# Raw weight buffers and the order of the seven-product steps in the MLP of a hybrid decoder layer

## The chip, the cores and the metric

The kernel runs on one core of one Trainium2 chip. The metric is device time in microseconds (us), smaller is better. The time before is 1105.0 us, the median of three runs (1101.55 to 1105.72).

A core has a matrix engine (PE in the profile; its weight loads are shown as PEld), three engines for elementwise work (DVE, the vector engine; ACT, the scalar engine; POOL), and SP, which here only issues DMA transfers from the chip's memory into SBUF. Every engine runs its own list of instructions strictly in the order of that list; engines wait for each other with semaphores. Matmul results go to PSUM, which has eight banks of 128 x 512 float32.

## The reference, cut to what matters

One decoder layer over 256 tokens of width 2048 in float32. The mixer (a Mamba-2 part and a sparse attention part between one input and one output projection) comes first; the change touches only what follows it:

```
u = rmsnorm(x, g_mlp) @ w_up                  # 256 x 2048 @ 2048 x 8192
return x + jnp.square(jax.nn.relu(u)) @ w_down  # 256 x 8192 @ 8192 x 2048
```

## The kernel before, in words

**Precise products.** Every float32 matrix is split into a rounded high part and a remainder, and a product is three matmuls: high by high, low by high, high by low (`three`, L186 to L192). Weights come from memory as a *raw* tile of 512 KB (128 partitions x 1024 values); ACT casts it to the high part (L144) and DVE subtracts to get the low part (L145). Both parts lie in one tile of the tag `w2`, which has `WB = 5` buffers; raw tiles have `RB = 4`. A raw buffer is free for the next load when DVE has subtracted; a `w2` buffer is free when PE has used it.

**Stages of the MLP.** The 8192 hidden columns are 32 groups of 256, worked off in three parts of 11, 11 and 10 groups (`PARTS`). For each part `up` computes the hidden values (PE line L230, "acc<-x2x,w" in the profile), squares them and splits them into `uh` and `ul`; then `down` multiplies them by `w_down`, in two halves `j` of 1024 output columns each. A half is a loop over the part's groups; one pass is a *step* here. A step needs two raw tiles (the quarters b11, b21 and b12, b22 of a 256 x 1024 block of `w_down`) and accumulates a 2 x 2 grid of PSUM banks.

**Plain and seven-product steps.** A plain step has eight products of 128x128 by 128x512, so 24 matmuls. In the steps listed in `SEVEN` Strassen's scheme (in Winograd's form) is used: seven products, 21 matmuls. For it POOL forms four combinations of the raw quarters (L852 to L855, one after another, one of them in place in the second raw tile); ACT then casts and DVE subtracts the two raw tiles (L860, L861) and the three other combinations, tile `t` (L863, L864), which become tile `wt`. `SEVEN = {2, 4, 6}` gives three such steps in each half, 18 of the 64 steps. Four products of a seven-product step go to four more banks (p1, p5, p6, p7); behind the last such step of a half ACT copies p1 (L913) and DVE adds these banks into the residual `xr` (L886 and L915 to L921). The eight banks are two tags of four, and the next half uses them the other way round: its grid takes the banks of p1, p5, p6 and p7.

**Order.** The order of PE's instructions is the order of the program text. For the other engines a scheduler sets it by a model of costs; everything inside `tc.high_priority(offset=HP)`, which holds the loads, casts, subtractions and combinations of weights, is pulled far ahead of its place. A buffer's reuse makes waits in that order: a load waits for the subtraction that frees its raw buffer, a cast for the matmul that frees its `w2` buffer.

**The start of the MLP.** The last residual of the mixer is transposed on PE (L694, tile ps_sr) and split by ACT (L697) and DVE (L698) into `x2x` while the first product of `up` already runs; ACT also squares the rows into scratch tiles (`junk`, L787). When the mixer's scratch pool `mid` is closed, the pool `mlp` takes its place in SBUF.

Of the kernel before, what the change touches and what calls it, by code (L numbers as in the profile page):

```python
# [9 lines left out]
F32 = mybir.dt.float32  # L10
F32R = mybir.dt.float32r
I32 = mybir.dt.int32
AF = mybir.ActivationFunctionType
OP = mybir.AluOpType
AX = mybir.AxisListType

P = 128
# [10 lines left out]
HP = 600  # L28
WARM = 9
WB = 5  # L30
RB = 4


SPARE = 64
SHIFT = 16
# [7 lines left out]
FIRST_W = 32  # L43


PARTS = (0, 11, 22, 32)
SEVEN = {2, 4, 6}

A11, A21, A12, A22 = range(4)
S3, S1, S2, S4 = 1, 4, 5, 6  # L50
# [34 lines left out]
def hymba_kernel(ctx: ExitStack, tc: tile.TileContext, xn, xt, w_in, w_out, w_up, w_down, vcol, vrow, out):  # L85
    nc = tc.nc
# [39 lines left out]
        return vc[:, VC[name] + i:VC[name] + i + 1]  # L126


    def operands(src, n, load=None, shift=0, parts=2):

        pitch = (n + 63) // 64 * 64
        with tc.high_priority(offset=HP):
            raw = wts.tile([P, parts, pitch], F32, name="raw", tag="raw", bufs=RB)
            both = wts.tile([P, 2 * parts * pitch + SPARE], F32R, name="w2", tag="w2", bufs=WB)
            hi, lo = (both[:, shift + i * parts * pitch:shift + (i + 1) * parts * pitch]
                      .rearrange("p (k c) -> p k c", k=parts)[:, :, :n] for i in range(2))
            src = src.rearrange("p (k c) -> p k c", k=parts)
            step = parts if load is None else 1
            for i in range(0, parts, step):
                s = slice(i, i + step)  # L140
                nc.sync.dma_start(raw[:, s, :n], src[:, s])
                if load is not None:
                    load()
                nc.scalar.copy(hi[:, s], raw[:, s, :n])  # L144
                nc.vector.tensor_tensor(lo[:, s], raw[:, s, :n], hi[:, s].bitcast(F32), op=OP.subtract)  # L145
        return hi, lo
# [663 lines left out]


    mlp = ctx.enter_context(tc.tile_pool(name="mlp", bufs=2))

    def up(h, tag):

# [18 lines left out]
            u.append((uh, ul))  # L834
        return u

    def weights(j, g, seven):


        if not seven:  # L840
            ops = [operands(w_down[2 * j + c, g], 512, shift=SHIFT) for c in range(2)]
            return [[(ops[c][0][:, k], ops[c][1][:, k]) for c in range(2)] for k in range(2)]
        with tc.high_priority(offset=HP):
            raws = []
            for c in range(2):
                raws.append(wts.tile([P, 2, 512], F32, name="raw", tag="raw", bufs=RB))
                nc.sync.dma_start(raws[c], w_down[2 * j + c, g].rearrange("p (k c) -> p k c", k=2))
            both = mlp.tile([P, 2 * 3 * 512 + SPARE], F32R, name="wt")
            th, tl = (both[:, SHIFT + i * 1536:SHIFT + (i + 1) * 1536].rearrange("p (k c) -> p k c", k=3) for i in range(2))
            t = mlp.tile([P, 3, 512], F32, name="t", bufs=1)  # L850

            nc.gpsimd.tensor_tensor(t[:, 0], raws[1][:, 1], raws[1][:, 0], op=OP.subtract)  # L852
            nc.gpsimd.tensor_tensor(raws[1][:, 0], raws[1][:, 0], raws[0][:, 0], op=OP.subtract)  # L853
            nc.gpsimd.tensor_tensor(t[:, 1], raws[1][:, 1], raws[1][:, 0], op=OP.subtract)  # L854
            nc.gpsimd.tensor_tensor(t[:, 2], raws[0][:, 1], t[:, 1], op=OP.subtract)  # L855
            ops = []
            for raw in raws:
                w2 = wts.tile([P, 2 * 2 * 512 + SPARE], F32R, name="w2", tag="w2", bufs=WB)
                hi, lo = (w2[:, SHIFT + i * 1024:SHIFT + (i + 1) * 1024].rearrange("p (k c) -> p k c", k=2) for i in range(2))
                nc.scalar.copy(hi, raw)  # L860
                nc.vector.tensor_tensor(lo, raw, hi.bitcast(F32), op=OP.subtract)  # L861
                ops.append((hi, lo))
            nc.scalar.copy(th, t)  # L863
            nc.vector.tensor_tensor(tl, t, th.bitcast(F32), op=OP.subtract)  # L864
        pick = lambda o, k: (o[0][:, k], o[1][:, k])
        (b11, b21), (t1, b22) = ([pick(o, k) for k in range(2)] for o in ops)
        t3, t2, t4 = (pick((th, tl), k) for k in range(3))
        return b11, b21, b22, t1, t2, t3, t4

    def down(h, u, tags):  # L870
        pairs = len(u)
        marked = SEVEN
        for j in range(2):
# [18 lines left out]
            kept = []  # L892
            for g in range(pairs):
                seven = g in marked
                w = weights(j, PARTS[h] + g, seven)
                if seven:
                    b11, b21, b22, t1, t2, t3, t4 = w
                    new = ps7 is None
# [10 lines left out]
                    go(acc[1][0], u[g], A22, t4, False)  # L909
                    if done:  # L910

                        s1 = mlp.tile([P, 512], F32, name="s1", bufs=1)
                        nc.scalar.copy(s1, p1)  # L913
                        add(0, half[0], p1)
                        nc.vector.tensor_tensor(s1, s1, p6, op=OP.add)  # L915
                        s2 = mlp.tile([P, 512], F32, name="s2", bufs=1)
                        nc.vector.tensor_tensor(s2, s1, p7, op=OP.add)
                        add(1, half[0], s2)
                        nc.vector.tensor_tensor(s1, s1, p5, op=OP.add)
                        add(0, half[1], s1)  # L920
                        nc.vector.tensor_tensor(s2, s2, p5, op=OP.add)  # L921
                        add(1, half[1], s2)
# [87 lines left out]
```

## Time and profile before

One execution was profiled. Its own time was 1102.39 us, its span 1100.6 us.

| what | number |
|---|---|
| three runs, median | 1105.0 us |
| the profiled execution | 1102.39 us, span 1100.6 us |
| PE busy | 1070.3 us, 97% |
| DVE, ACT, POOL busy | 746.4, 551.0, 123.5 us |
| mean granted TensorE clock | 0.990 |
| down stages, from first to last matmul | about 501.9 to 628.0, 745.3 to 873.2 and 979.9 to 1097.0 us |

How to read it: in rows of waits the first name is who waited, behind the arrow what ended the wait, then the total, the number of times and the longest, in us. In rows of groups: line, engine, operation, output<-inputs, shapes, count, then busy us and the mean ns of one, then the idle time of the engine before them with its releaser. In a timeline: start, duration, engine, line, operation, and in brackets the idle time before it. In rows of stretches: the stretch, its length, then busy time and count of instructions of each engine asked for, the granted clock (1.00 is full), the share of the DMA engines in use, GB/s. Matmuls overlap: one of 512 columns is shown with 0.38 us, though the next starts 0.22 us after it. The ends of matmuls are modelled.

### The profile page before, as it was taken

How to read it: one execution, taken by the hardware profiler on the slowest of the kernel's cores; microseconds unless marked ns; L12 is line 12 of the kernel's file. 1: busy time of each engine (PE TensorE's matmuls, PEld its weight loads, DVE VectorE, ACT ScalarE, POOL GpSimd, SP SyncE). 2: the span in 40 equal slices, each digit the busy share in tenths (PEclk: the TensorE clock that was granted, in tenths of full speed). 3: DMA queues.
4: the chain of work that ended last, by engine and by line, in shares of the span. 5: the costliest groups of instructions: out<-in, count | busy, mean ns of one | idle time of the engine just before them, and what ended most of it. 6: DMA issues, size and time to landing. Idle time of an engine off the chain costs nothing.

```text
span 1100.6 us, 15648 instructions
## 1 busy us (share of the span) xinstructions
PE 1070.3 (97%) x5962; PEld 938.7 (85%) x5962; DVE 746.4 (68%) x1066; ACT 551.0 (50%) x749; POOL 123.5 (11%) x102
## 2 busy tenths in 40 slices
PE   9999999999999999999898999999998999998988
PEld 8999998888888898988686889897786888987876
DVE  6787997687665576764674767765665767754846
ACT  7755555567654554553544445544344445544433
POOL 0020000221000000003123000004123000023140
PEclk9999999999999999999999999999899999999999
DMA  9865437544565556664554766663554666645753
GB/s 329 261 213 182 158 105 241 172 135 135 165 236 187 187 185 201 196 197 150 186 178 161 242 207 195 194 207 134 192 186 169 226 202 192 198 147 172 239 163 115
DMA packets 63611, 207.41 MB, mean 188 GB/s; under 512 B 7088, under 2 KB 11440, under 8 KB 63536
## 3 DMA queue, kind: packets, MB, share of 16 engines
q1 hardware_dynamic: 63392, 206.36, 57.5%
q8 instruction: 47, 0.77, 0.3%
q14 instruction: 28, 0.23, 0.1%
q10 hardware_dynamic: 144, 0.05, 0.0%
HBM read 204.29 MB, written 2.10 MB: 188 GB/s over the span
## 4 chain that ended last, share of the span: by engine, by line
PE 73%; POOL 9%; DMA 5%; DVE 5%; issue 4%; ACT 4%; POOLq 0%; ACTq 0%; DVEq 0%
PE acc L230 29%; PE acc L192 10%; PE acc L209 10%; PE acc L189 10%; PE acc L191 10%; DMA raw<-in_w_down 5%; POOL raw L853 2%; DVE w L861 2%; POOL t L854 2%; POOL t L852 2%; POOL t L855 2%; ACT wt L863 2%; DVE w L145 2%; ACT w L144 2%; PE ps_y L610 1%
## 5 line engine op out<-in xcount | busy, mean ns | idle before, releaser
L145 DVE TENSOR_TENSOR w<-raw,w 128x1024 fp32r<-128x1024 f32 (+3 forms) x364 | 420.2, 1166 | 204.0 <-ACT w L144 203.1
L144 ACT CAST w<-raw 128x1024 fp32r<-128x1024 f32 (+3 forms) x364 | 357.5, 993 | 335.8 <-PE acc L192 104.7
L230 PE MATMUL acc<-x2x,w 128*128 128x512 f32 (+2 forms) x2053 | 343.0, 327 | 0.0
L230 PEld LDWEIGHTS acc<-x2x,w 128*128 128x128 f32 x2053 | 307.9, 188 | 34.4
L192 PE MATMUL acc<-w,uh 128*128 128x512 f32 (+1 forms) x444 | 171.9, 387 | 15.6 <-DVE w L861 15.6
L189 PE MATMUL acc<-w,uh 128*128 128x512 f32 (+5 forms) x459 | 171.4, 379 | 10.0 <-ACT w L860 10.0
L191 PE MATMUL acc<-w,ul 128*128 128x512 f32 (+1 forms) x444 | 169.4, 382 | 0.0
L209 PE MATMUL acc<-hx,w 128*128 128x256 f32 (+1 forms) x978 | 115.0, 277 | 0.0
L192 PEld LDWEIGHTS acc<-w,uh 128*128 128x128 f32 x444 | 83.7, 189 | 35.2 <-DVE w L861 21.0
L209 PEld LDWEIGHTS acc<-hx,w 128*128 128x128 f32 x978 | 112.7, 188 | 0.0
L189 PEld LDWEIGHTS acc<-w,uh 128*128 128x128 f32 x459 | 86.2, 188 | 29.2 <-ACT w L860 14.4
L864 DVE TENSOR_TENSOR wt<-t,wt 128x1536 fp32r<-128x1536 f32 x18 | 31.7, 1759 | 114.9 <-ACT wt L863 114.9
L852 POOL TENSOR_TENSOR t<-raw 128x512 f32<-128x512 f32 x18 | 24.7, 1373 | 716.5 <-DMA raw<-in_w_down 669.1
L191 PEld LDWEIGHTS acc<-w,ul 128*128 128x128 f32 x444 | 83.7, 188 | 14.4
L863 ACT CAST wt<-t 128x1536 fp32r<-128x1536 f32 x18 | 26.5, 1474 | 128.9 <-POOL t L855 128.9
L189 PE MATMUL acc<-w,hx 128*128 128x512 f32 (+3 forms) x228 | 83.9, 371 | 0.0
L191 PE MATMUL acc<-w,hx 128*128 128x512 f32 (+1 forms) x224 | 80.9, 361 | 0.0
L192 PE MATMUL acc<-w,hx 128*128 128x512 f32 (+1 forms) x224 | 80.7, 360 | 0.0
L189 PEld LDWEIGHTS acc<-w,hx 128*128 128x128 f32 x228 | 43.0, 189 | 6.1 <-issue 0.7
L191 PEld LDWEIGHTS acc<-w,hx 128*128 128x128 f32 x224 | 42.4, 189 | 5.9 <-issue 0.7
L192 PEld LDWEIGHTS acc<-w,hx 128*128 128x128 f32 x224 | 42.2, 189 | 6.0 <-DVE w L145 0.4
L861 DVE TENSOR_TENSOR w<-raw,w 128x1024 fp32r<-128x1024 f32 x36 | 46.1, 1279 | 0.2 <-ACT w L860 0.2
(229 smaller groups left out, 1033.3 us busy)
## 6 DMA issues: line engine op xcount, KB each, us to landing
raw<-in_w_up SPq DMA_DIRECT2D x128, 512.0 KB, 4.1
raw<-in_w_down SPq DMA_DIRECT2D x128, 512.0 KB, 4.3
raw<-in_w_in SPq DMA_DIRECT2D x72, 512.0 KB, 3.5
raw<-in_w_out SPq DMA_DIRECT2D x32, 512.0 KB, 3.3
raw<-in_w_in SPq DMA_DIRECT2D x16, 256.0 KB, 5.2
raw<-in_w_in SPq DMA_DIRECT2D x16, 152.0 KB, 5.2
raw<-in_w_in SPq DMA_DIRECT2D x8, 304.0 KB, 3.2
xT<-in_xt SPq DMA_DIRECT2D x8, 256.0 KB, 5.2
```

What stands on the lines that cost most here:

```text
L144: nc.scalar.copy(hi[:, s], raw[:, s, :n])
L145: nc.vector.tensor_tensor(lo[:, s], raw[:, s, :n], hi[:, s].bitcast(F32), op=OP.subtract)
L189: nc.tensor.matmul(go(out[:, i:j]), ah, go(wh[:, i:j]), start=first and i == 0, stop=False, skip_group_check=True)
L191: nc.tensor.matmul(go(out), al, go(wh), start=False, stop=False, skip_group_check=True)
L192: nc.tensor.matmul(go(out), ah, go(wl), start=False, stop=last, skip_group_check=True)
L209: nc.tensor.matmul(acc[:, c, at:at + n], w[:, 0, s], x[:, fr:fr + n], start=(i + k + j == 0), stop=(i >= 2 and k == 7 and j == len(todo) - ...
L230: nc.tensor.matmul(walk(out[:, at:at + n]), w[:, 0, s], walk(x[:, at:at + n]), start=(i < 2 and k + j == 0), stop=(i >= 2 and k == 7 and j ...
L852: nc.gpsimd.tensor_tensor(t[:, 0], raws[1][:, 1], raws[1][:, 0], op=OP.subtract)
L853: nc.gpsimd.tensor_tensor(raws[1][:, 0], raws[1][:, 0], raws[0][:, 0], op=OP.subtract)
L861: nc.vector.tensor_tensor(lo, raw, hi.bitcast(F32), op=OP.subtract)
L863: nc.scalar.copy(th, t)
L864: nc.vector.tensor_tensor(tl, t, th.bitcast(F32), op=OP.subtract)
```

## The change

- `SEVEN` becomes {2, 5, 8}, so two plain steps stand between seven-product steps. `PARTS` becomes (0, 10, 21, 32): parts of 10, 11 and 11 groups. There are still 18 seven-product and 46 plain steps.
- Once the pool `mlp` exists, raw tiles are taken in turn from the old four buffers and from four new ones (tag `rawm`) in `mlp`.
- `weights` is divided. `combine` loads the two raw tiles of a seven-product step and forms the combinations on POOL; it is called one step ahead, before the loads of the plain step in front. `combined` does the casts and subtractions, at the step itself.
- To make room `wt` has one buffer in place of two, and `s1`, `s2` take the two buffers of `up`'s tile `r`.

```diff
-PARTS = (0, 11, 22, 32)
-SEVEN = {2, 4, 6}
+PARTS = (0, 10, 21, 32)
+SEVEN = {2, 5, 8}
...
+    mlp_pool = []
+    taken = [0]
+
+    def raw_tile(parts, pitch):
+
+        taken[0] += 1
+        pool, tag = (mlp_pool[0], "rawm") if mlp_pool and taken[0] % 2 else (wts, "raw")
+        return pool.tile([P, parts, pitch], F32, name="raw", tag=tag, bufs=RB)
+
     def operands(src, n, load=None, shift=0, parts=2):
...
-            raw = wts.tile([P, parts, pitch], F32, name="raw", tag="raw", bufs=RB)
+            raw = raw_tile(parts, pitch)
...
     mlp = ctx.enter_context(tc.tile_pool(name="mlp", bufs=2))
+    mlp_pool.append(mlp)
...
+    def combine(j, g):
+
         with tc.high_priority(offset=HP):
             raws = []
             for c in range(2):
-                raws.append(wts.tile([P, 2, 512], F32, name="raw", tag="raw", bufs=RB))
+                raws.append(raw_tile(2, 512))
                 nc.sync.dma_start(raws[c], w_down[2 * j + c, g].rearrange("p (k c) -> p k c", k=2))
...
             t = mlp.tile([P, 3, 512], F32, name="t", bufs=1)
...
+        return raws[0], raws[1], t
+
+    def combined(raws):
+
+        ops = []
+        with tc.high_priority(offset=HP):
             for raw in raws:
...
+                    both = mlp.tile([P, 2 * 3 * 512 + SPARE], F32R, name="wt", bufs=1)
...
                 nc.scalar.copy(hi, raw)
                 nc.vector.tensor_tensor(lo, raw, hi.bitcast(F32), op=OP.subtract)
...
-                w = weights(j, PARTS[h] + g, seven)
+
+                if g + 1 in marked:
+                    ahead = combine(j, PARTS[h] + g + 1)
+                w = combined(ahead) if seven else plain(j, PARTS[h] + g)
...
-                        s1 = mlp.tile([P, 512], F32, name="s1", bufs=1)
+                        s1, s2 = (mlp.tile([P, 7, P], F32, name="r")[:, :4].rearrange("p k t -> p (k t)")
+                                  for _ in range(2))
                         nc.scalar.copy(s1, p1)
                         add(0, half[0], p1)
                         nc.vector.tensor_tensor(s1, s1, p6, op=OP.add)
-                        s2 = mlp.tile([P, 512], F32, name="s2", bufs=1)
```

The change moves instructions at three places of which the prediction speaks. Numbers in names tell buffers and tiles apart.

**ACT, the second seven-product step of a part's first half** (step 4 before, step 5 now). Before; w2_5240 and w2_5245 are the plain step 3, w2_5283, wt_5277 and w2_5286 the seven-product step 4, w2_5313 the plain step 5:

```order
L144 CAST w2_5240<-raw_5239 128x1024
L144 CAST w2_5245<-raw_5244 128x1024
L860 CAST w2_5283<-raw_5273 128x1024
L863 CAST wt_5277<-t_5278 128x1536
L860 CAST w2_5286<-raw_5275 128x1024
L144 CAST w2_5313<-raw_5312 128x1024
```

Now; w2_5144 and w2_5149 are step 3, w2_5187 and w2_5192 step 4, the next three step 5, w2_5251 the plain step 6:

```order
L153 CAST w2_5144<-raw_5143 128x1024
L153 CAST w2_5149<-raw_5148 128x1024
L153 CAST w2_5187<-raw_5186 128x1024
L153 CAST w2_5192<-raw_5191 128x1024
L879 CAST w2_5220<-raw_5177 128x1024
L879 CAST wt_5226<-t_5181 128x1536
L879 CAST w2_5223<-raw_5179 128x1024
L153 CAST w2_5251<-raw_5250 128x1024
```

The cast to `wt` still stands between the two other casts of its step, but now two plain steps lie ahead of it; it waits for POOL as before, and also for PE's last use of the one `wt` buffer, in step 2.

**SP and ACT, the start of the MLP.** raw_4002 to raw_4090 are the four tiles of `up`'s first product; raw_4150, 4171, 4192 and 4213 those of its second. SP before:

```order
L141 DMA raw_4090<-in_w_up 128x1024 [waits DMAHW1_49,DVE_49]
L141 DMA raw_4150<-in_w_up 128x1024 [waits DMAHW2_49,DVE_49]
L141 DMA raw_4171<-in_w_up 128x1024 [waits DMAHW3_49,DVE_49]
L141 DMA raw_4192<-in_w_up 128x1024 [waits DMAHW4_49,DVE_49]
L141 DMA raw_4213<-in_w_up 128x1024 [waits DMAHW5_49,DVE_49]
```

SP now; the ACT semaphore that raw_4150 waits for is reached by the second of the two squarings (junk2_4067, L796):

```order
L150 DMA raw_4090<-in_w_up 128x1024 [waits DMAHW1_49,DVE_49]
L150 DMA raw_4171<-in_w_up 128x1024 [waits DMAHW2_49,DVE_49]
L150 DMA raw_4213<-in_w_up 128x1024 [waits DMAHW3_49,DVE_49]
L150 DMA raw_4267<-in_w_up 128x1024 [waits DMAHW4_49,DVE_49]
L150 DMA raw_4309<-in_w_up 128x1024 [waits DMAHW5_49,DVE_49]
L150 DMA raw_4150<-in_w_up 128x1024 [waits PE_49,Activation_49,Pool_49]
```

ACT now, from these squarings on:

```order
L796 ACTIVATE junk2_4065,ss2_3350<-xr_3345 128x512
L796 ACTIVATE junk2_4067,ss2_3350<-xr_3345 128x512
L706 ACTIVATE x2x_3547<-ps_sr_4024,vc_86 128x256 x2
L153 CAST w2_4151<-raw_4150 128x1024
L153 CAST w2_4172<-raw_4171 128x1024
L153 CAST w2_4193<-raw_4192 128x1024
L706 ACTIVATE x2x_3547<-ps_sr_4047,vc_86 128x256 x2
```

The first loads into the new buffers, raw_4150 and raw_4192, stand behind the end of the mixer's scratch pool, and on ACT the last two slices of `x2x` (from ps_sr_4047) now stand behind the casts of these two tiles. Before, all four slices stood ahead of the cast of raw_4192. DVE has the same order.

**DVE, the change of half in the first part** (10 groups; behind its last seven-product step there is one plain step, where there were four before). acc_5117 to acc_5120 are p1, p5, p6 and p7, r_5357 and r_5358 are s1 and s2; wt_5493 belongs to step 2 of the next half:

```order
L901 SCALAR_TENSOR_TENSOR xr_3345<-acc_5117,rs4_4113,xr_3345 128x512
L154 TENSOR_TENSOR w2_5416<-raw_5415,w2_5416 128x1024
L154 TENSOR_TENSOR w2_5454<-raw_5453,w2_5454 128x1024
L934 TENSOR_TENSOR r_5357<-r_5357,acc_5119 128x512
L935 TENSOR_TENSOR r_5358<-r_5357,acc_5120 128x512
L880 TENSOR_TENSOR wt_5493<-t_5448,wt_5493 128x1536
L901 SCALAR_TENSOR_TENSOR xr_3345<-r_5358,rs4_4113,xr_3345 128x512
L937 TENSOR_TENSOR r_5357<-r_5357,acc_5118 128x512
L939 TENSOR_TENSOR r_5358<-r_5358,acc_5118 128x512
```

The subtraction to `wt` of the next half stands in the middle of the chain that frees p5's bank; before, nothing stood between these adds.

More of the change, by code (lines that the diff above doesn't have):

```diff
@@ L835, in up, with plain @@
         return u
[L837 to L842, printed above, removed]
+    def plain(j, g):
+        ops = [operands(w_down[2 * j + c, g], 512, shift=SHIFT) for c in range(2)]
+        return [[(ops[c][0][:, k], ops[c][1][:, k]) for c in range(2)] for k in range(2)]
+    def combine(j, g):
         with tc.high_priority(offset=HP):
@@ L845, in weights @@
             for c in range(2):
-                raws.append(wts.tile([P, 2, 512], F32, name="raw", tag="raw", bufs=RB))
+                raws.append(raw_tile(2, 512))
                 nc.sync.dma_start(raws[c], w_down[2 * j + c, g].rearrange("p (k c) -> p k c", k=2))
-            both = mlp.tile([P, 2 * 3 * 512 + SPARE], F32R, name="wt")
-            th, tl = (both[:, SHIFT + i * 1536:SHIFT + (i + 1) * 1536].rearrange("p (k c) -> p k c", k=3) for i in range(2))
             t = mlp.tile([P, 3, 512], F32, name="t", bufs=1)
@@ L855, in weights @@
             nc.gpsimd.tensor_tensor(t[:, 2], raws[0][:, 1], t[:, 1], op=OP.subtract)
-            ops = []
+        return raws[0], raws[1], t
+    def combined(raws):
+        ops = []
+        with tc.high_priority(offset=HP):
             for raw in raws:
-                w2 = wts.tile([P, 2 * 2 * 512 + SPARE], F32R, name="w2", tag="w2", bufs=WB)
-                hi, lo = (w2[:, SHIFT + i * 1024:SHIFT + (i + 1) * 1024].rearrange("p (k c) -> p k c", k=2) for i in range(2))
+                n = raw.shape[1]
+                if n == 2:
+                    both = wts.tile([P, 2 * 2 * 512 + SPARE], F32R, name="w2", tag="w2", bufs=WB)
+                else:
+                    both = mlp.tile([P, 2 * 3 * 512 + SPARE], F32R, name="wt", bufs=1)
+                hi, lo = (both[:, SHIFT + i * n * 512:SHIFT + (i + 1) * n * 512].rearrange("p (k c) -> p k c", k=n)
+                          for i in range(2))
                 nc.scalar.copy(hi, raw)
                 nc.vector.tensor_tensor(lo, raw, hi.bitcast(F32), op=OP.subtract)
[L862 to L867, printed above, removed]
+                ops.append([(hi[:, k], lo[:, k]) for k in range(n)])
+        (b11, b21), (t1, b22), (t3, t2, t4) = ops
         return b11, b21, b22, t1, t2, t3, t4
```

## The prediction

> **What bounds the kernel now.** I read the page's engine totals first, then who waited for whom, then the down stages alone.
>
> ```profile
> PE 1070.3 (97%) x5962; PEld 938.7 (85%) x5962; DVE 746.4 (68%) x1066; ACT 551.0 (50%) x749; POOL 123.5 (11%) x102
> PE acc L192 <- DVE w L861: 15.6, 13, 1.3
> PE acc L189 <- ACT w L860: 10.0, 8, 2.2
> ACT wt L863 <- POOL t L855: 128.9, 18, 8.1
> ```
>
> PE is the bound, and nearly all of its idle time (25.6 us) stands in 21 waits for the weights of seven-product steps. A busy PE is not a PE at its pace, though, so I measure the stages by their length: the three stretches from the first to the last matmul of a down stage, and the pace of matmuls where nothing waits.
>
> ```profile
> 501.90:628.00 126.10, 117.49 (x519) 96.62 (x517) 79.04 (x76) 54.32 (x54) 32.57 (x24) 0.99 0.55 180
> 745.30:873.20 127.90, 119.97 (x519) 98.56 (x517) 79.10 (x77) 54.43 (x54) 31.89 (x23) 0.96 0.54 180
> 979.90:1097.00 117.10, 108.12 (x481) 89.14 (x479) 69.86 (x71) 45.93 (x46) 30.56 (x24) 0.97 0.49 165
> ...
> 617.23 0.39 PE L189 MATMUL acc<-w,uh 128*128 128x512 f32 x1
> ...
> 627.28 0.38 PE L189 MATMUL acc<-w,uh 128*128 128x512 f32 x1
> ```
>
> Between the two last rows lie 45 matmuls: 10.05/45 = 0.2233 us each. A part of 11 groups has 2 x (8 x 24 + 3 x 21) = 510 matmuls, 113.9 us, and 0.3 for cut first ones: 114.2. The part of 10 has 462, of which 24 are half as wide: 103.4. The stages sum to 371.1 (about 370.8 from first start to last end) where PE's pace gives 331.8: **39 us are lost there.** 25.6 is the idle time. Each of 21 restarts costs about 0.27 more (5.7): the wait is counted from an end that lies 0.16 behind the next start, and the first matmul takes 0.11 longer (0.49 below against 0.38). The remaining 7 to 8 us are the clock:
>
> ```profile
> 588.18 0.49 PE L189 MATMUL acc<-w,uh 128*128 128x512 f32 x1 [0.77 <-ACT w L860]
> 590.17 0.49 PE L192 MATMUL acc<-w,uh 128*128 128x512 f32 x1 [1.28 <-DVE w L861]
> ...
> 590.00:591.00 1.00, 0.83 (x4) 0.97 0.00 0
> 591.00:592.00 1.00, 1.00 (x4) 0.50 0.81 283
> 592.00:593.00 1.00, 1.00 (x3) 0.50 0.83 287
> ```
>
> Just behind this pair of waits the granted clock falls to 0.50, for some 3.4 us. I take it that the waits do it and that it goes with them; the other answer is a rival below.
>
> Why PE waits is read in the chain of waits and SP's timeline.
>
> ```profile
> 576.91 0.33 SPq L847 DMA_DIRECT2D raw<-in_w_down  x1
> ...
> 579.15 1.15 DVE w L861
> ...
> 580.34 1.27 POOL t L852
> ...
> 584.39 1.29 POOL t L855
> ...
> 587.09 1.04 ACT w L860
> ...
> 593.63 1.26 POOL t L852
> ```
>
> It is a loop: a raw buffer comes free late, the load takes 3.4 us (576.91 to 580.3), POOL 5.4 (580.34 to 585.7), then ACT casts `wt` and, only behind it, the second tile, which PE needs early. POOL starts its next turn 13.3 us later (580.34 to 593.63); PE's work in a turn, a seven-product and a plain step, takes (21 + 24) x 0.2233 = 10.0.
>
> **The change part by part.** Prices come from these groups.
>
> ```profile
> L145 DVE TENSOR_TENSOR w<-raw,w 128x1024 fp32r<-128x1024 f32 x324 | 396.5, 1234 | 195.9 <-ACT w L144 195.1
> L144 ACT CAST w<-raw 128x1024 fp32r<-128x1024 f32 x324 | 336.4, 1047 | 326.7 <-PE acc L192 104.7 <-issue 100.5 <-PE acc L230 50.3
> L864 DVE TENSOR_TENSOR wt<-t,wt 128x1536 fp32r<-128x1536 f32 x18 | 31.7, 1759 | 114.9 <-ACT wt L863 114.9
> L863 ACT CAST wt<-t 128x1536 fp32r<-128x1536 f32 x18 | 26.5, 1474 | 128.9 <-POOL t L855 128.9
> L853 POOL TENSOR_TENSOR raw<-raw 128x512 f32<-128x512 f32 x18 | 25.7, 1426 | 1.4
> L886 DVE SCALAR_TENSOR_TENSOR xr<-s,rs,xr 128x512 f32<-128x512 f32 x18 | 13.0, 748 | 0.2
> L917 DVE TENSOR_TENSOR s<-s,acc 128x512 f32<-128x512 f32 x6 | 4.1, 687 | 0.2
> ```
>
> *Matmuls:* 46 x 24 + 18 x 21 before and after; no gain or loss.
>
> *Buffers, look-ahead, distance:* a load now waits for the subtraction of four steps earlier, not two, and POOL starts one step sooner. Inside a half, count from the start of step 2. Its seven products end at 4.7 and step 5 begins at 15.3. The cast to `wt` for step 5 waits for 4.7 (one buffer), though POOL was done long before; 1.5 + 1.8 later the low part is there, at 8. The second tile's `w2` buffer is free at 8.7 (three quarters through step 3), so its low part is ready at 11. PE needs both between 16 and 18. At least 5 us of cover; if it goes, every us over it is a stall. Then `t` is free at 8, POOL works for step 8 until 13.4, or 16.7 if it is slowed as below, and ACT wants it at 20. So the loop is gone inside a half: **-39 us** (bounds -39 and, if one drop of the clock remains, -37).
>
> *The start of the MLP* is a new wait. These rows are ACT's second squaring, DVE's last slice of `x2x`, PE's stream, and the landing times:
>
> ```profile
> 385.60 0.19 ACT L787 ACTIVATION_READ_ACCUMULATOR junk<-xr 128x1 f32 x1
> 390.51 0.48 DVE L698 SCALAR_TENSOR_TENSOR x2x<-ps_sr,vc,x2x 128x256 fp32r<-128x256 f32 x1
> 388.39 9.96 PE L230 MATMUL acc<-x2x,w 128*128 128x32 f32 x58
> raw<-in_w_up SPq DMA_DIRECT2D x13, 512.0 KB, 3.4
> ```
>
> raw_4150 and raw_4192 are issued behind 385.8 and land 3.4 and, with 1.6 for another 512 KB, 5 us later: 389.2 and 390.8. ACT then casts three tiles (389.4 to 392.5); the third, on DVE, ends at 394.1 behind two others of 1.2. Only then come the last two slices: 0.5 each on DVE, 394.6, and behind a pass over ACT 395.5. PE reaches the first of them 21 matmuls behind 388.39, nine until the next weight tile and twelve in it, at 0.17 (9.96/58): 391.9. It stands 2.7 + 0.6: **+3.3 us** (bounds 0, if the loads land at once, and 6, if at 4.1 us and crossed), and perhaps a clock drop, +0.8 (0 to 1.7). Behind it the second product's tiles are all late by the same and no more.
>
> *The change of half in the first part.* PE needs p5's bank 1.3 us into the next half, 11.3 from the start of step 8 (4.7 + 5.3 + 1.3). That chain on DVE now holds the subtraction to `wt`. Its raw tiles take step 8's buffers. The second of these is cast when PE is three quarters through step 6, 6.7 ahead of step 8, and subtracted 2.3 later; the load lands some 4.3 later still, at about 0. POOL ends at 5.5, ACT at 7.4 with the semaphores between, DVE at 9.2; then 0.75 + 0.69 + 0.69 = 11.3. Just in time, if POOL runs undisturbed. But POOL and DVE disturb each other:
>
> ```profile
> 565.34 1.29 POOL L852 TENSOR_TENSOR t<-raw 128x512 f32<-128x512 f32 x1 [29.00 <-DMA raw<-in_w_down]
> 566.71 2.15 POOL L853 TENSOR_TENSOR raw<-raw 128x512 f32<-128x512 f32 x1
> ...
> 559.82 1.23 DVE L145 TENSOR_TENSOR w<-raw,w 128x1024 fp32r<-128x1024 f32 x1 [1.32 <-ACT w L144]
> ...
> 565.41 2.30 DVE L145 TENSOR_TENSOR w<-raw,w 128x1024 fp32r<-128x1024 f32 x1
> ```
>
> Where they meet, POOL takes 2.15 for 1.29 and DVE 2.30 for 1.23. [...] Three of four combinations slowed by 0.87 and the subtraction held up make p5 free at about 14: **+2** (0 to 4). In the other two parts two plain steps follow step 8, 5.3 us more cover; two more changes, together **+1** (0 to 3). At the end of the last half the same cover holds.
>
> *From up to down.* ACT now meets the cast to `wt` for step 2 ahead of two casts of `up`'s last product. Count from the start of the product before it; a product is four weight tiles of 2.7 us (16 matmuls at 0.17), and casts run five tiles ahead. The raw buffer that step 2 waits for is freed at 0, its load lands at 4.3, POOL ends at 10, the cast to `wt` at 11.5, the cast behind it at 12.6; on DVE that is 13.3 and 14.6. PE wants this tile, the third of the last product, at 16. ACT stands for some 6 us, but 1.4 us of cover is left. Three crossings, **+1.5** (0 to 6: 2 each if POOL is slowed). Scratch in `r` costs nothing: `up` is over, or a product of 10 us away.
>
> Sum: 1100.6 - 39 + 3.3 + 0.8 + 2 + 1 + 1.5 = 1070.2; the profiled execution lies 1.8 above its span: **1072**. It was itself 2.6 below the median shown, inside the runs' 1101.55 to 1105.72.
>
> **Rivals.** *The lock between POOL and DVE decides.* In the before POOL mostly works while ACT and DVE stand; now it works against a full stream. DVE's 228.0 us in the down stages plus 72 combinations x 1.07 is 305 of 332 us, 92%, and at each end of a half the adds come on top. Against: on average it fits, and weights are 2.5 steps ahead. If each of six halves loses 3 us: 1063.4 (1102.4 less 39) + 18 + 4.1 at the start + 1.5 at the crossings = 1087.
>
> *The clock drops are not the waits' doing* and stay: 7.5 us more, 1080. Against: each stands in or just behind a pair of waits, and long stretches without waits have none. [...]
>
> *It doesn't do what it says:* ACT still meets POOL unfinished at each of 18 `wt` casts and the loop reappears there, 39 us lost as before and 3.3 more at the start: 1106. It needs POOL 10 us later than I count; no combination took above 2.15.
>
> *Slower, by new places in SBUF:* `uh`, `ul` and `wt` lie elsewhere, and if that slowed the stage's matmuls, all 1482 would pay. For it: those on `wt` take longer even now.
>
> ```profile
> L189 PE MATMUL acc<-w,uh 128*128 128x512 f32 x421 | 162.8, 387 | 10.0 <-ACT w L860 10.0
> L189 PE MATMUL acc<-wt,uh 128*128 128x512 f32 x54 | 23.9, 443 | 0.0
> ...
> 515.47 0.38 PE L189 MATMUL acc<-wt,uh 128*128 128x512 f32 x1
> ...
> 517.45 0.38 PE L189 MATMUL acc<-w,uh 128*128 128x512 f32 x1
> ```
>
> 0.056 more on each is 83 us: 1155; it decides from 0.02 on, where it eats my 30. Against: in an undisturbed step the nine matmuls on `wt` take 1.98, 0.220 each. Their mean is long because the clock drops fall on them.
>
> **The numbers.** My forecast 0.67, the lock 0.21, the clock 0.03, no effect 0.04, slower 0.05. Forecast's own range 1063 (nothing lost) to 1082 (all upper bounds). The clock's 1080 lies in it. The range reaches to the lock, 1063 to 1091, and leaves out no effect and slower. A measurement here can tell about 0.5% from no change: faster 0.91 (the first three), same 0.04, slower 0.05.
>
> **What would show it.** Right: no wait of PE for L879/L880's products inside halves, clock 1.00 in the down stages, stages near 105, 115 and 115 us; one wait of PE near 392 for the low part of `x2x`; POOL means rising to 1.5 or more. Wrong: PE waits at every change of half (the lock), ACT idle in front of `wt` by 5 us or more (the loop), a pace above 0.23 in clean stretches (places).

## The result, and the profile after

The changed kernel takes 1065.29 us (median of 4 runs, 1064.19 to 1066.81) against 1104.4 us before (4 runs): a ratio of 0.965, 95% interval 0.9625 to 0.9675. The profiled execution is the one of 1066.81 us, with a span of 1065.0.

These are the engine totals of the changed kernel's page:

```profile
PE 1057.3 (99%) x5962; PEld 936.6 (88%) x5962; DVE 785.3 (74%) x1066; ACT 555.8 (52%) x749; POOL 151.4 (14%) x102
```

All its waits of PE, by what ended them:

```profile
PE acc L239 <- DVE x2x L707: 2.7, 2, 2.4
PE ps_w L254 <- POOL ones L249: 1.3, 1, 1.3
PE acc L198 <- ACT hx L277: 0.3, 1, 0.3
```

And its three down stages as stretches:

```profile
499.00:601.00 102.00, 102.00 (x469) 87.22 (x469) 84.02 (x71) 52.96 (x53) 36.00 (x20) 1.00 0.66 217
719.00:831.00 112.00, 112.00 (x515) 95.67 (x514) 91.73 (x77) 55.58 (x55) 35.93 (x20) 1.00 0.64 215
949.00:1061.00 112.00, 112.00 (x523) 96.02 (x523) 89.31 (x76) 51.59 (x51) 35.93 (x20) 1.00 0.54 182
```

The 21 waits for seven-product weights are gone. In the down stages PE is busy for the whole stretch, at the full clock. One new wait stands in the list, for `x2x`, and it is in the place that the prediction named: the start of the MLP. The timeline there shows ACT's casts, then a late slice of `x2x`, then PE:

```profile
390.01 2.00 ACT L153 CAST w<-raw 128x1024 fp32r<-128x1024 f32 x2 [0.49 <-DMA raw<-in_w_up]
392.54 1.04 ACT L153 CAST w<-raw 128x1024 fp32r<-128x1024 f32 x1 [0.52 <-DMA raw<-in_w_up]
393.49 0.47 ACT L706 ACTIVATE x2x<-ps_sr,vc 128x256 fp32r<-128x256 f32 x1
395.29 0.79 PE L239 MATMUL acc<-x2x,w 128*128 128x512 f32 x2 [2.44 <-DVE x2x L707]
396.31 1.01 PE L239 MATMUL acc<-x2x,w 128*128 128x512 f32 x2 [0.24 <-DVE x2x L707]
```

The two stretches around it show the granted clock, which falls to 0.50 behind the stall:

```profile
392.16:395.57 3.41, 0.97 (x6) 0.63 (x5) 2.91 (x4) 1.72 (x3) 0.00 (x0) 1.00 0.72 249
395.57:398.98 3.41, 3.17 (x10) 2.30 (x10) 1.02 (x2) 1.49 (x3) 0.00 (x0) 0.50 0.85 286
```

Where the 35.6 us between the spans (1100.6 and 1065.0) come from, by the first matmul of each stage in the two traces (the last stage up to its last matmul's start): the down stages last 101.96, 112.51 and 112.58 us, together 327.0 instead of 370.6, so -43.6. The up stages last 115.27, 117.45 and 117.45, together 350.2 instead of 342.9 for the same 32 groups, so +7.3. What lies ahead of the MLP is 0.7 longer, what lies behind it the same.

What POOL and DVE cost each other is there too. These are the groups of a seven-product step in the changed kernel: subtraction and cast of its raw tiles, POOL's second and fourth combination, cast to `wt`.

```profile
L880 DVE TENSOR_TENSOR w<-raw,w 128x1024 fp32r<-128x1024 f32 x36 | 56.4, 1566 | 20.5 <-ACT w L879 18.4 <-DMA raw<-in_w_down 1.7
L862 POOL TENSOR_TENSOR raw<-raw 128x512 f32<-128x512 f32 x18 | 32.4, 1800 | 1.4
L864 POOL TENSOR_TENSOR t<-raw,t 128x512 f32<-128x512 f32 x18 | 33.5, 1859 | 1.4
L879 ACT CAST wt<-t 128x1536 fp32r<-128x1536 f32 x18 | 26.5, 1474 | 39.8 <-POOL t L864 27.0 <-PE acc L201 12.8
```

POOL's operations take 1.8 us on average where the second took 1.43 before; DVE is busy 39 us longer than before and POOL 28, with the same instructions. None of it reaches PE. ACT's wait for POOL in front of `wt` fell from 128.9 us to 27.0.

### The profile page after: what moved, and what is told of

It is laid out like the page before. It is cut to its first block, busy times and chain, and to the rows that moved or that the text cites. A ratio compares the mean times of both kernels' runs of the same rounds, so it can differ in the third digit from the quotient of the medians.

```text
span 1065.0 us, 15655 instructions
## 1 busy us (share of the span) xinstructions
PE 1057.3 (99%) x5962; PEld 936.6 (88%) x5962; DVE 785.3 (74%) x1066; ACT 555.8 (52%) x749; POOL 151.4 (14%) x102
## 4 chain that ended last, share of the span: by engine, by line
PE 98%; DMA 1%; ACT 0%; DVE 0%; SPq 0%; issue 0%; ACTq 0%
PE acc L239 32%; PE acc L198 17%; PE acc L200 17%; PE acc L201 17%; PE acc L218 10%; PE ps_y L619 1%; DMA raw<-in_w_up 1%; PE ps_l L657 0%; PE ps_o L682 0%; PE ps_sr L703 0%; DMA xT<-in_xt 0%; PE ps_s L510 0%; PE ps_s L509 0%; PE ps_dec L610 0%; PE ps_pt L674 0%; DVE w L154 0%
## 5 line engine op out<-in xcount | busy, mean ns | idle before, releaser
L154 DVE TENSOR_TENSOR w<-raw,w 128x1024 fp32r<-128x1024 f32 (+3 forms) x364 | 439.4, 1218 | 197.0 <-ACT w L153 195.2
L153 ACT CAST w<-raw 128x1024 fp32r<-128x1024 f32 (+3 forms) x364 | 359.6, 993 | 330.4 <-PE acc L201 139.3
L239 PE MATMUL acc<-x2x,w 128*128 128x512 f32 (+2 forms) x2053 | 347.6, 330 | 2.7 <-DVE x2x L707 2.7
L198 PE MATMUL acc<-w,uh 128*128 128x512 f32 (+5 forms) x459 | 168.6, 373 | 0.0
L201 PE MATMUL acc<-w,uh 128*128 128x512 f32 (+1 forms) x444 | 168.1, 379 | 0.0
L880 DVE TENSOR_TENSOR w<-raw,w 128x1024 fp32r<-128x1024 f32 x36 | 56.4, 1566 | 20.5 <-ACT w L879 18.4
L879 ACT CAST w<-raw 128x1024 fp32r<-128x1024 f32 x36 | 37.7, 1046 | 41.9 <-PE acc L201 36.8
```

The lines of the kernel that those rows point to most:

```text
L198: nc.tensor.matmul(go(out[:, i:j]), ah, go(wh[:, i:j]), start=first and i == 0, stop=False, skip_group_check=True)
L201: nc.tensor.matmul(go(out), ah, go(wl), start=False, stop=last, skip_group_check=True)
L239: nc.tensor.matmul(walk(out[:, at:at + n]), w[:, 0, s], walk(x[:, at:at + n]), start=(i < 2 and k + j == 0), stop=(i >= 2 and k == 7 and j ...
```

## The experiments

All times stand against the kernel before, run on the same chip. "PE waits" are those in the MLP, added up from each timeline; a few tenths that the groups of waits below hold beyond them lie in the mixer.

| kernel | us | ratio, 95% interval | PE waits, us |
|---|---|---|---|
| the change | 1065.3 | 0.965 (0.9625 to 0.9675) | 2.7 |
| distance alone | 1105.4 | 0.997 (0.994 to 1.000) | 24.1 |
| the change with four raw buffers | 1087.3 | 0.982 (0.978 to 0.986) | 17.7 |
| the change without look-ahead | 1069.5 | 0.967 (0.962 to 0.971) | 5.2 |
| the change without distance | 1065.1 | 0.962 (0.958 to 0.965) | 3.4 |
| eight buffers alone | 1062.9 | 0.9615 (0.959 to 0.964) | 2.7 |
| the change, new buffers late | 1059.6 | 0.9587 (0.956 to 0.961) | 0 |
| the same, six buffers | 1063.6 | 0.962 (0.958 to 0.966) | 2.8 |
| the same, combinations on DVE | 1065.4 | 0.963 (0.960 to 0.967) | 3.6 |
| eight buffers alone, late | 1059.8 | 0.9576 (0.955 to 0.960) | 0 |
| the change, three more POOL operations a step | 1100.2 | 0.995 (0.993 to 0.997) | 22.5 |
| four seven-product steps, POOL | 1068.6 | 0.967 (0.964 to 0.970) | 8.0 |
| four seven-product steps, DVE | 1057.2 | 0.956 (0.953 to 0.959) | 0.3 |

### Distance alone

The kernel before with the new places of the seven-product steps, nothing else:

```diff
-PARTS = (0, 11, 22, 32)
-SEVEN = {2, 4, 6}
+PARTS = (0, 10, 21, 32)
+SEVEN = {2, 5, 8}
```

> The kernel before with one part of the change alone: seven-product steps 2, 5 and 8 instead of 2, 4 and 6 (and the parts' borders 10 and 21 that go with them); four raw buffers, no look-ahead. My theory (the raw buffer that is freed late is the cause, so a longer distance only lets the weights recover between two turns): the start of the MLP costs nothing, as in the kernel before; about a third to a half of the 39 us of the down stages is lost still, since the raw tiles of each seven-product step are still behind the same four buffers; 1075 to 1092 us, with waits of PE for the casts and subtractions of the halves left. Rival (distance is all that matters: the loop of 13.3 us a turn needs two turns in a row to show): no waits in the down stages, and without the 5 us at the start of the MLP 1060 to 1064 us, faster than the whole change.

1105.4 us: the rival is out, and my theory had the direction but too much effect: I gave distance half of the loss or more, and it gave 0.3%. The timeline of one seven-product step (lines of the kernel before) shows why a longer distance does not help:

```profile
516.96 1.28 POOL L855 TENSOR_TENSOR t<-raw,t 128x512 f32<-128x512 f32 x1
518.27 1.47 ACT L863 CAST wt<-t 128x1536 fp32r<-128x1536 f32 x1 [7.09 <-POOL t L855]
519.65 1.04 ACT L860 CAST w<-raw 128x1024 fp32r<-128x1024 f32 x1
521.45 1.22 DVE L861 TENSOR_TENSOR w<-raw,w 128x1024 fp32r<-128x1024 f32 x1
522.73 0.49 PE L192 MATMUL acc<-w,uh 128*128 128x512 f32 x1 [1.26 <-DVE w L861]
```

ACT, which works in order, stands 7.09 us in front of `wt`, and the step's second tile is cast behind it. It stands there for POOL at all 18 steps, 124.5 us together, against 128.9 before. That happens in each such step by itself; no second turn is needed for it. So my picture of a loop of 13.3 us against 10.0 was too narrow: the chain inside one step is late already.

### Eight buffers alone

The changed kernel with the old places of the steps, and the combinations asked for in the step itself. Against the kernel before this leaves the eight buffers (and one `wt` buffer and the scratch in `r`, which make room for them):

```diff
-PARTS = (0, 10, 21, 32)
-SEVEN = {2, 5, 8}
+PARTS = (0, 11, 22, 32)
+SEVEN = {2, 4, 6}
-                if g + 1 in marked:
-                    ahead = combine(j, PARTS[h] + g + 1)
+                if seven:
+                    ahead = combine(j, PARTS[h] + g)
```

> The kernel before with eight raw buffers alone (and the one wt buffer that makes room for them): steps 2, 4 and 6, combinations asked for in the step itself. If the buffers carry the whole gain, as the runs without look-ahead and with the old distance say: no waits for the halves, the stall near 392 us as in the changed kernel, and at most 3 us at the changes of half: 1062 to 1069 us. If look-ahead and distance stand in for each other, so that either was enough beside the buffers but not neither: the chain of load 3.4, POOL 5.4 to 7.5, cast 1.5 and subtraction 1.8 us shows at the halves again, 1072 to 1090 us.

1062.9 us: the buffers carry the whole gain. Its only waits in the MLP are the 2.7 us for `x2x`. ACT still stands in front of `wt` for POOL, 12 times and 45.9 us together, but PE feels none of it: with eight buffers the loads and combinations run early enough whichever step asks for them. What makes room for the buffers was not run alone; the next version has it with four buffers, and waits.

### Taking one part out of the change

Each of these undoes one part of the change. Four raw buffers:

```diff
-        pool, tag = (mlp_pool[0], "rawm") if mlp_pool and taken[0] % 2 else (wts, "raw")
+        pool, tag = wts, "raw"
```

> The changed kernel with all raw tiles from the four old buffers (the four of the MLP's own are left out); look-ahead and distance stay. My theory: the stall near 392 us goes (its load waited for a new buffer), which gives back 3.3 us and 1.7 us of halved clock; in exchange the raw tiles of a seven-product step now hold two of four buffers for a whole step longer, so the plain steps behind them load late: 1066 to 1085 us, with PE waits for casts of plain tiles in the down stages. Rival (the buffers are not needed once step and distance are changed): no waits in the down stages, 1060 to 1063 us.

1087.3 us, just above the range of my theory. The up stages lose nothing, the stall at the start is gone as expected, and the down stages last 352.1 us instead of 327.0:

```profile
PE acc L198 <- DVE r L939: 9.0, 1, 9.0
PE acc L201 <- DVE w L154: 7.3, 9, 1.5
PE acc L198 <- ACT w L153: 2.4, 2, 1.6
```

The waits are now for plain tiles (L153, L154), which load behind the two that the look-ahead holds, as the theory had it, and 9.0 us at the first part's change of half, which I had not expected. With distance alone the down stages last 367.8 us, 15.6 more: look-ahead, with the rewriting that comes with it, is worth that much where buffers are short.

No look-ahead:

```diff
-                if g + 1 in marked:
-                    ahead = combine(j, PARTS[h] + g + 1)
+                if seven:
+                    ahead = combine(j, PARTS[h] + g)
```

> The changed kernel with the combinations asked for in the seven-product step itself (no look-ahead); eight buffers and distance stay. My theory (buffers are the cause; the scheduler runs loads and combinations as early as buffers allow, whatever step asks for them): POOL still begins several us ahead of the step, at most a few short waits, 1065 to 1070 us. Rival (the look-ahead is what hides the chain load 3.4, POOL 7.5, cast 1.5, subtraction 1.8 us): waits of some us at each of the 18 steps, 1075 to 1090 us.

1069.5 us, as my theory had it. In the down stages PE waits at the three changes of half, for p5's bank, and nowhere else:

```profile
550.63 0.49 PE L198 MATMUL acc<-w,uh 128*128 128x512 f32 x1 [1.25 <-DVE r L939]
776.89 0.50 PE L198 MATMUL acc<-w,uh 128*128 128x512 f32 x1 [0.56 <-DVE r L939]
1008.51 0.50 PE L198 MATMUL acc<-w,uh 128*128 128x512 f32 x1 [0.56 <-DVE r L939]
```

With the restarts and with a slower pace, behind these 2.4 us and in the first stage ahead of them too (the last section comes to it), the down stages last 333.2 instead of 327.0. The spans (1067.4 and 1065.0) lie less apart, since this run's stall for `x2x` did not halve the clock (1.00 in both stretches around it; the last section has them) and its first up stage is 3.9 shorter. So one and the same stall cost 3.2 to 3.4 us in the two versions whose clock stayed full (this one and eight buffers alone), and 7.3 in the change.

No distance (the first four lines of the diff of eight buffers alone):

> The changed kernel with the old places of the seven-product steps (2, 4 and 6, borders 11 and 22); eight buffers and look-ahead stay. My theory: the loop is cut by the buffers, a turn of two steps has 19 us of PE work against about 16 us of chain, so no waits in the down stages: 1064 to 1070 us, as the whole change. [...]

1065.1 us, as the whole change. Distance is worth 0.3% with four buffers and nothing with eight.

### The start of the MLP

The new buffers are used only from the fourth product of the MLP on, so that no early load waits for the mixer's scratch pool:

```diff
-    mlp_pool.append(mlp)
...
         for j in range(PARTS[h + 1] - PARTS[h]):
+            if h == 0 and j == 3:
+                mlp_pool.append(mlp)
```

> The changed kernel, with the MLP's own raw buffers used only from the fourth product of the MLP on; until then all raw tiles go to the four old ones. My theory: the first load into a new buffer no longer waits for the end of the second squaring, so the casts ahead of x2x's last slices are not held: the waits for x2x near 395 us (2.44 and 0.24 us) and the clock's drop behind them (1.7 us) go, 1059 to 1062 us against 1065 of the changed kernel. Rival (ACT is late there by its own work: it ends the squarings at 385.9 and has four slices and three casts to do): the wait stays at 2 us or more, 1064 to 1066 us.

1059.6 us, and no wait for `x2x`. The first up stage takes 108.0 us instead of 115.3. Of these 7.3 us (the medians lie 5.7 apart) the stall with its restarts is 3.2 and the halved clock 1.7; the rest, 2.4, is a slower pace that PE keeps behind the stall, with no wait and the clock at 1.00. These are the same 90 us of the changed kernel and of this one:

```profile
400.00:490.00 90.00, 90.00 (x528) 79.56 (x527) 56.01 (x70) 42.10 (x55) 6.14 (x4) 1.00 0.56 182
```

```profile
400.00:490.00 90.00, 90.00 (x541) 80.97 (x540) 60.42 (x76) 43.52 (x57) 6.12 (x4) 1.00 0.60 185
```

528 matmuls against 541. The last two edits together, eight buffers alone and used late, are the smallest that should bring everything:

> The kernel before with eight raw buffers alone (steps 2, 4 and 6, no look-ahead), the new ones used from the fourth product on: the smallest change that should bring everything. Theory: 1057 to 1061 us, the same as look-ahead and distance with the late buffers (1059.6). Rival (without the stall near 395 us to slow PE down, the first down stage finds its weights later, since nothing is asked for in advance): waits in the halves of part 0, 1062 to 1070 us.

1059.8 us: look-ahead and distance add nothing that these runs can tell. How many buffers are needed was asked by giving the late version two new ones instead of four:

```diff
-        return pool.tile([P, parts, pitch], F32, name="raw", tag=tag, bufs=RB)
+        return pool.tile([P, parts, pitch], F32, name="raw", tag=tag, bufs=RB if pool is wts else 2)
```

> The kernel with the late new buffers, with two of them instead of four: six raw buffers. With four (and the look-ahead) 1087 us, with eight 1060 us. Theory (each missing buffer makes a load wait for a cast; POOL holds two of them for a step): most of the gain is there with six, 1060 to 1068 us, with single waits at the changes of half. Rival (the ring has to hold two whole steps beyond the seven-product step, that is eight): 1070 to 1085 us.

1063.6 us. Six are enough for every step inside a half; the one wait is 2.8 us for p5's bank at the first part's change of half, with a slower pace behind it.

### POOL against DVE

Is there cover left? Three of the four combinations are done twice, with the same results:

```diff
             nc.gpsimd.tensor_tensor(t[:, 0], raws[1][:, 1], raws[1][:, 0], op=OP.subtract)
+            nc.gpsimd.tensor_tensor(t[:, 0], raws[1][:, 1], raws[1][:, 0], op=OP.subtract)
...
+            nc.gpsimd.tensor_tensor(t[:, 1], raws[1][:, 1], raws[1][:, 0], op=OP.subtract)
...
+            nc.gpsimd.tensor_tensor(t[:, 2], raws[0][:, 1], t[:, 1], op=OP.subtract)
```

> The changed kernel with three of the four combinations done twice (seven POOL operations a step instead of four; the results are the same). POOL's chain grows from about 7.5 to about 13 us a step, and takes that much more of the time that DVE and POOL share. Theory (eight buffers and the look-ahead leave the chain some 16 us from the load to the use): waits appear only at the changes of half and the first steps, below 10 us in all, 1065 to 1077 us. Rival (the shared time is used up already, DVE and POOL together 92% to 94% of the down stages): each of the 18 steps loses 3 us or more, 1110 us and above.

1100.2 us: nearer to the rival's price, but at my theory's places. PE's 22.5 us of waits stand at the ends of `up`, at and just behind the changes of half, at the start and at one seven-product step, ten in all; behind five of these places the clock is halved.

```profile
PE acc L201 <- DVE w L154: 6.2, 2, 3.1
PE acc L198 <- DVE r L942: 5.3, 1, 5.3
PE acc L239 <- DVE w L154: 4.1, 3, 1.5
```

Seven of the ten, 17.3 us, come just behind a long stand of ACT in front of `wt`. The one at 794.92, from POOL's last combination on:

```profile
787.30 1.28 POOL L867 TENSOR_TENSOR t<-raw,t 128x512 f32<-128x512 f32 x1
788.61 1.47 ACT L882 CAST wt<-t 128x1536 fp32r<-128x1536 f32 x1 [10.10 <-POOL t L867]
790.12 1.76 DVE L883 TENSOR_TENSOR wt<-t,wt 128x1536 fp32r<-128x1536 f32 x1 [6.82 <-ACT wt L882]
794.92 0.80 PE L201 MATMUL acc<-w,uh 128*128 128x512 f32 x1 [3.13 <-DVE w L154]
```

ACT stands 10.10 us, DVE 6.82 with nothing to subtract, and the plain tiles that PE needs next are cast behind `wt`. In all ACT stands there 17 times, 111.1 us. So it is first the length of POOL's chain that costs here, through ACT's order, and not time that DVE lacks: DVE is idle ahead of these seven waits for 2.7 to 8.1 us. What I gave 0.21 as the lock shows too: four subtractions of 2.3 us instead of 1.2 stand close ahead of the wait at 553.73, and it makes POOL's chain longer (2.15 us for 1.28 where the two meet). This run doesn't separate the two prices. The change has room for its POOL work, but not for nearly twice as much. Doing the combinations on DVE itself, in the version with late buffers, takes POOL out and keeps the work:

```diff
-            nc.gpsimd.tensor_tensor(t[:, 0], raws[1][:, 1], raws[1][:, 0], op=OP.subtract)
+            nc.vector.tensor_tensor(t[:, 0], raws[1][:, 1], raws[1][:, 0], op=OP.subtract)
...
```

(The other three combinations are moved in the same way.)

> The kernel with the late new buffers, its four combinations a step moved from POOL to DVE (72 operations of some 0.6 us by DVE's 1.23 us for 128x1024: 45 us more on DVE, none on POOL). Theory (POOL's operations cost DVE about as much in shared time, 39 us over the program, as doing the work itself): DVE stays near 780 us busy, the chain of combinations falls from 7.5 to 2.5 us, no waits: 1057 to 1062 us, as with POOL. Rival (DVE works in order: a combination that waits for its load holds the subtractions behind it): waits for subtractions in the down stages, 1064 to 1080 us.

1065.4 us. Groups of this kernel: its subtraction of a seven-product step's raw tiles, its first combination; and, from its timeline, its only wait in the down stages.

```profile
L881 DVE TENSOR_TENSOR w<-raw,w 128x1024 fp32r<-128x1024 f32 x36 | 44.0, 1222 | 11.1 <-ACT w L880 10.2
L862 DVE TENSOR_TENSOR t<-raw 128x512 f32<-128x512 f32 x18 | 12.4, 692 | 13.1 <-DMA raw<-in_w_down 12.9
```

```profile
549.44 0.50 PE L198 MATMUL acc<-w,uh 128*128 128x512 f32 x1 [3.63 <-DVE r L940]
```

With POOL idle the subtraction takes 1.22 us, and 1.57 on average beside POOL in the changed kernel. DVE's total is 790 us here, and 786 in the late version, where POOL does the 72 combinations: POOL's work beside it costs DVE about as much as doing that work. Both expectations were half right: the steps have no waits, and the order does hold one thing, the chain of p5 at the first change of half, where DVE does three of the next half's combinations and three of its subtractions between the additions.

### Four seven-product steps

With the late buffers, four such steps in each half, and one raw buffer less, since more `u` tiles need the room. First with POOL, then with the combinations on DVE as above:

```diff
-SEVEN = {2, 5, 8}
+SEVEN = {1, 3, 5, 7}
...
-        return pool.tile([P, parts, pitch], F32, name="raw", tag=tag, bufs=RB)
+        return pool.tile([P, parts, pitch], F32, name="raw", tag=tag, bufs=RB if pool is wts else 3)
```

> The changed kernel with the late new buffers and with four seven-product steps a half instead of three (steps 1, 3, 5 and 7; one raw buffer less, seven, since the larger u tiles need the room). Six more seven-product steps save three matmuls of 0.221 us each: 4.0 us of PE. Theory (the weights have time to spare): 1055 to 1059 us, no waits in the down stages. Rival (24 combinations instead of 18 and 33% more lock time on DVE, step 1 right behind the up stage, whose ACT and DVE work is still queued): waits at the first seven-product step of each part of 2 to 5 us, 1060 to 1070 us.

> The kernel with four seven-product steps a half (steps 1, 3, 5 and 7, seven raw buffers, late new buffers), its combinations on DVE instead of POOL. If the time that DVE and POOL share is what made four steps slower than three (the profile with POOL has DVE busy 86% in the down stages), it falls away here: 1054 to 1059 us. If it is DVE's total work, whoever does the combinations, or the one raw buffer less: 1064 to 1075 us again, with waits for DVE's subtractions.

With POOL 1068.6 us, with DVE 1057.2. The middle down stage of the first and of the second:

```profile
721.70:834.90 113.20, 112.41 (x511) 94.84 (x510) 97.46 (x79) 56.59 (x55) 46.91 (x25) 1.00 0.62 207
```

```profile
714.50:825.70 111.20, 111.20 (x511) 95.06 (x510) 94.39 (x101) 57.96 (x55) 0.00 (x0) 1.00 0.62 206
```

111.2 against 112.5 with three such steps: the six matmuls saved in a stage, 6 x 0.22 = 1.3, are there. With POOL they are lost to waits (8.0 us in all), their restarts and the slower pace behind them: its three down stages last 336.5 us, with DVE 324.3. The up stages last 346.0 in both, the second at a slow pace (120.6 against 117.5). So it was POOL, not the buffer that is missing: these two kernels differ in nothing else. Whether its slower chain or the time that it takes from DVE does more isn't shown. Ahead of the wait at 496.00 three of DVE's subtractions take 2.2 to 2.3 us; the waits for `wt` (2.2 us) come behind ACT, which stands for POOL 18 times, 54.3 us. The best kernel here is this last one; from the late versions of the change (1059.6 and 1059.8) its interval does not set it apart.

## Why the prediction was right, and where it was off

1072 was forecast, 1065.3 measured, inside the range and inside the forecast's own one. That it is so near is partly luck: the sum had 4.6 us too little gain in the down stages and 4.5 us of costs that measured nothing, but also 3.2 us too little at the start and 0.7 ahead of the MLP. The lower bound, 1063 with nothing lost, was none: the late version takes 1059.6.

**The 39 us of the down stages** went, and by the mechanism named: waits, restarts and clock drops together. But the term was too small. The stages are 43.6 shorter. The pace of 0.2233 that I took for PE's own, from 617 to 627 us, is a slowed one: the undisturbed step that I quoted against the rival of new places had 0.220, and the changed kernel has 0.2200 in all three stages. 1482 matmuls x 0.0033 = 4.9 us, about the difference of 327.0 to my 331.8. I had both numbers and did not ask why they differed.

**What did it** I put down to buffers, look-ahead and distance together, against a loop that gains on PE turn by turn. That picture is the step that failed here: distance alone, which gives the loop a plain step more to recover, took 2.9 us off the down stages, because the chain inside one step is late by itself. The runs say buffers; look-ahead helps where buffers are short, or at a change of half with only one or two plain steps ahead of it; distance hardly helps.

**The start of the MLP** was forecast as 3.3 of waiting and 0.8 of clock; it is 3.2 and 1.7, and 2.4 of slower pace that was in no term. The mechanism was right, since the late version loses the wait.

**The change of half**, +2 and +1, and **the crossings**, +1.5, measured nothing. For the first part the step that failed is "Its raw tiles take step 8's buffers". They take step 7's (the two loads are issued at 528.25 and 529.38, as the subtractions of its plain tiles end), which come earlier, and POOL starts some 6 us sooner than I counted:

```profile
534.76 1.29 POOL L861 TENSOR_TENSOR t<-raw 128x512 f32<-128x512 f32 x1 [8.77 <-DMA raw<-in_w_down]
...
540.59 2.27 POOL L864 TENSOR_TENSOR t<-raw,t 128x512 f32<-128x512 f32 x1
...
545.40 1.47 ACT L879 CAST wt<-t 128x1536 fp32r<-128x1536 f32 x1 [0.99 <-PE acc L201]
548.12 1.75 DVE L880 TENSOR_TENSOR wt<-t,wt 128x1536 fp32r<-128x1536 f32 x1
...
551.04 0.68 DVE L939 TENSOR_TENSOR r<-r,acc 128x512 f32<-128x512 f32 x1
...
552.41 0.38 PE L198 MATMUL acc<-w,uh 128*128 128x512 f32 x1
```

The subtraction to `wt` does sit inside the chain of additions, as forecast, and p5 is free at 551.7. PE reaches it 53.1 us into the stage, at the last row. (The version on DVE shows which row it is: there this matmul waits, it was due at 545.65, and the stage begins at 492.55.) That is 0.7 us to spare. The runs without look-ahead, with six buffers and on DVE wait at just this place (1.25, 2.85 and 3.63 us), so the estimate of "just in time" was good and its sign luck.

**The rival of the lock** did not decide, yet POOL's means rose to 1.4 to 1.9 us and the cover is thinner than I argued: 54 more operations, which took POOL's total from 151 to 260 us, cost 35 us. But 17.3 of the 22.5 us of waits there came through ACT's stand in front of `wt`, not through the time that DVE loses, which is what I had priced as the lock. By what means the two engines slow each other no run shows; in the changed kernel's trace POOL's combinations take 1.28 us where no work of DVE overlaps them (10 of 72) and 1.83 us on average where some does. **The clock** drops went with the waits. **New places in SBUF**: refuted, a matmul on `wt` now takes 380 ns on average, like one on any other tile.

One sign that I named was wrong: "ACT idle in front of `wt` by 5 us or more" was to show the loop. ACT still stands there for POOL five times, up to 6.8 us, and PE feels none of it. Three of the five are the crossings from up to down, with 6.3 to 6.8 us, where the prediction itself counted some 6.

Sum with the measured terms: 1100.6 - 43.6 + 7.3 + 0.7 = 1065.0, and 1.8 above the span.

## What to carry to other kernels

When an in-order engine stands in front of one long chain, give the loads more buffers before changing the order of the work: with room, the scheduler brings everything early by itself. Buffers in a pool that replaces a closed one wait for the closed one's last user, so let the first loads use the old ones. And take an engine's pace from a stretch with no wait ahead of it, not only none inside.

## What the runs showed of the chip

**The clock.** Stalls of equal size halve the clock in some traces and not in others: the wait for `x2x` did so in the changed kernel (0.97 of 3.41 us busy, above, then 0.50), but not without look-ahead:

```profile
391.40:394.81 3.41, 1.50 (x10) 1.09 (x8) 3.38 (x4) 2.17 (x3) 0.00 (x0) 1.00 0.79 269
394.81:398.22 3.41, 2.50 (x13) 2.02 (x14) 1.09 (x4) 1.72 (x3) 0.00 (x0) 1.00 0.91 299
```

In the traces of the kernel before and of the change every drop to 0.50 starts at a multiple of 3.413 us from the others of its trace (590.95, 782.10, 846.95, 1007.38, 1065.40 and 1099.54 us, where 782.10 to 846.95 is 19 of them; 395.57 and 1064.58 us). It lasts 3.41 us, the one at 782.10 twice that; the last of each trace goes on to its end. With the MLP cut into such stretches, PE stood 1.92, 1.83, 2.10, 1.74 and 1.88 us of the 3.41 ahead of the five drops in the MLP before, and 2.44 in the change. That does not decide by itself: the same 1.74 us (from 1000.55 us on, before) left the clock at 1.00, and so did the 1.91 us of the first row above. These are two stretches of the kernel before, the first ahead of a drop and the second in it:

```profile
587.54:590.95 3.41, 1.49 (x6) 0.98 (x7) 3.41 (x3) 3.41 (x4) 0.00 (x0) 1.00 0.21 84
590.95:594.36 3.41, 3.41 (x10) 2.63 (x9) 2.57 (x3) 0.03 (x1) 0.77 (x1) 0.50 0.89 277
```

The version on DVE waits longer, 3.63 us, and keeps its clock. In the two stretches that hold the wait PE stood 1.77 and 1.86 us:

```profile
544.17:547.58 3.41, 1.64 (x8) 1.06 (x6) 3.41 (x5) 0.74 (x1) 0.00 (x0) 1.00 0.21 37
547.58:550.99 3.41, 1.55 (x7) 1.31 (x8) 3.41 (x6) 0.00 (x0) 0.00 (x0) 1.00 0.76 269
```

That the clock stays because the wait is cut in two there is my estimate from these rows and the drops above.

**PE's pace.** The same matmuls run at different paces with no wait and the clock at 1.00. The up stages of the version with four steps on DVE, the second and the third:

```profile
605.00:705.00 100.00, 100.00 (x587) 88.39 (x586) 71.43 (x96) 51.15 (x66) 0.00 (x0) 1.00 0.60 190
840.00:940.00 100.00, 100.00 (x602) 90.01 (x601) 74.02 (x99) 51.89 (x67) 0.00 (x0) 1.00 0.62 195
```

587 against 602 of the same work, 3.1 us in a stage. For 512 columns the levels were 0.2200 (all three down stages of the change), 0.2227 to 0.2233 (the kernel before, behind its waits) and 0.2283 us (the version on DVE, behind 549.44 us). Every down stage began at 0.2200. A pace lasted until the next wait, the next change of stage, or a hitch too short for the list of waits: in the first down stage without look-ahead a weight load (PEld) stood 0.19 us for a subtraction, the matmul behind it came 12 ns late, and from there on the pace is 0.2233 up to the first wait, some 42 us later.

```profile
508.01 0.19 PEld L201 LDWEIGHTS acc<-w,uh 128*128 128x128 f32 x1 [0.19 <-DVE w L880]
508.08 0.42 PE L201 MATMUL acc<-w,uh 128*128 128x512 f32 x1
```

Behind a wait it was 0.2200 in 7 of the 24 stretches of down stages that I counted, 0.2283 in one, 0.2227 to 0.2233 in the others. In the profiled executions it cost distance alone 6.2 us in its up stages, more than the 2.9 that its down stages gained. What sets the level isn't known from these runs; no run here tried to set it.
